# Chunks 16 and 17 of the way down of two feed-forward steps: from plain products to a fifth group of seven block products

## The chip, the cores and the metric

The kernel runs on one core of one Trainium2 chip. The metric is the device time of one launch in microseconds. Three runs of the kernel before took 1115.5, 1116.13 and 1116.92 us; the median, 1116.13, is the time before.

## The reference

One step of a decoder layer over 576 rows: a prompt of 512 and eight samples of 8. All in fp32. The part that is changed is the half-weight feed-forward step, which stands first and last in the layer:

```python
def swiglu(x, w_gate, w_up, w_down):
    return (jax.nn.silu(x @ w_gate) * (x @ w_up)) @ w_down

x = x + 0.5 * swiglu(rmsnorm(x, ffn1_norm), ffn1_w_gate, ffn1_w_up, ffn1_w_down)
...   # input projection, RG-LRU heads, pooling heads, output projection, cross attention
x = x + 0.5 * swiglu(rmsnorm(x, ffn2_norm), ffn2_w_gate, ffn2_w_up, ffn2_w_down)
```

The model width is 1024 (8 blocks of 128), the hidden width 2816 (22 chunks of 128).

## The kernel before

Activations lie transposed: 128 features on the partitions, the 576 rows along the free axis, in two halves of 288. Every fp32 product is made of three products of rounded parts: an operand is split into a high part (a cast on the scalar engine, ACT, line 192) and a low part (the difference, on the vector engine, DVE, line 195), and high x high, high x low and low x high are added up in PSUM. So each weight block costs a load, a cast and a difference before the tensor engine (PE) can use it.

`ffn` (line 374) computes one feed-forward step. `head` is true in the first step. The *way up* makes the 22 hidden chunks, two or three of them plainly, the rest in a loop (line 816), chunk by chunk, by a scheme in which a 2x2 block product takes seven block products where the plain way takes eight. The seven are named 11, E, 22, F, G, 12 and H in the loop; each has twelve matrix products here (`product`, line 367). They accumulate in the PSUM tiles `pu`, `pc`, `pa`. `finish_chunk` (line 800) does the product 22 of a chunk in the middle of the next chunk, or after the loop for the last.

The *way down* multiplies the hidden chunks by `w_down` and adds the result to `x`. Its work is cut into *steps* in a queue (`steps`, line 485), and `fill()` takes one step from that queue behind each of the seven products of a chunk. One product of the way up and one step make what is called a period below. An explicit chain keeps the tensor engine's products in the order in which they are written; the other engines' orders come from a list scheduler that goes by the written order among what it takes to be ready.

For chunks 0 to 15, four groups of four chunks (`quick(g)`, line 629) also use seven block products for eight. In a group, pair `i` (0 to 15 over all groups) covers two output blocks; `depth` two means that the inner dimension of each block product is two chunk pairs deep: `put` makes 2 x 3 products. Its PSUM tiles are `dU`, `dC`, `dA` and `dD`, four banks under the tag `d`. The steps of a pair are `s11`, `sE`, `sF`, `s12`, `sH` and `sG` with `s22`. U takes up 11, is copied to A, takes up F, is copied to D, takes up H, is read out, takes up 22 and is read out again (`take`, line 641). Read-outs go into temporary tiles `add_e` (tag `acc`, one buffer) and `add_1`, `add_2` (tag `sq`, two buffers), and a DMA issued by GpSimd (POOL) adds them to `x` in place (lines 657, 684, 691). `ensure` (line 601) makes the split weight tiles `dh` and `dl` (three buffers) from the raw blocks in `td`, a ring of four slots, and from a fourth block in `t2`; `fetch_pair` (line 586) loads them through the queue of SyncE (SP). In the second step two sums of blocks have been formed ahead, in DRAM; in the first step DVE forms them (lines 613, 614).

The operands of the hidden side are in `pairs` (line 550): `build_a` and `build_b` make, of a pair of chunks, the seven splits that the groups need; `build_plain` makes one plain split of a chunk.

The last six chunks are plain: `PLAIN = (16, 2), (18, 4)`. `down(0)` covers chunks 16 and 17 and is put into the queue at chunk 18, behind the fourth group. It makes eight output blocks times two chunks, a step each, with six products (three parts, two halves) into `pd` (tag `d`). Its panels, 128 x 256, go through `fetch` and `make`. Sixteen steps of it run from the last filler of chunk 19 on. In the first step of the layer the last of them stands behind `finish_chunk` of chunk 21; in the second an additional `fill()` puts it ahead. `down(1)` then does chunks 18 to 21 after the loop, in the first step with the addition to `x` on DVE, in the second in a tail of its own that also makes the final norm. While `down(0)` does its block 7, it already makes panel 0 of the next one (`make(8)`).

Of the kernel before, what the change touches and what calls it, by code (L numbers as in the profile page):

```python
# [9 lines left out]
F32 = mybir.dt.float32  # L10
F32R = mybir.dt.float32r
# [5 lines left out]
P = 128  # L17
# [4 lines left out]
FFC = 22  # L22
STD = (3, 2)

FAST = 4
PLAIN = (16, 2), (18, 4)
NQ = DC // 2
OFFS = [0, P, 2 * P, 3 * P, T - P]
TA = T - P
# [41 lines left out]
def hybrid_step(ctx, tc, a):  # L71
    nc = tc.nc
    v, s, te = nc.vector, nc.scalar, nc.tensor
# [92 lines left out]
    for i in range(FAST * NQ):  # L166
        w = a["f2_d"][i // NQ, i % NQ].rearrange("p b k n -> p b (k n)")
# [21 lines left out]
    def split(hi, lo, src, scale=None):  # L189

        if scale is None:
            i = cast[0] = s.copy(hi, src)  # L192
            if first[0] is not None:
                after_(i, first[0])
            return v.tensor_tensor(out=lo, in0=src, in1=f(hi), op=ALU.subtract)  # L195
        s.activation(hi, src, AF.Copy, scale=scale)
        return v.scalar_tensor_tensor(out=lo, in0=src, scalar=scale, in1=f(hi), op0=ALU.mult, op1=ALU.subtract)
# [176 lines left out]
    def ffn(name, n, fp, turn, plain, head=False):  # L374

        wstd, wgu, wq, wd = (a[f"{name}_{q}"] for q in ("s", "gu", "d", "dp"))

        def single(tag, nm_):  # L380
            return now["ff"].tile([P, 512], F32, tag=tag, bufs={"u": 2, "d": 4}.get(tag, 1), name=nm_)
# [103 lines left out]
        steps = deque()  # L485
# [62 lines left out]
        raw, raw22, pairs, t2 = {}, {}, {}, {}  # L548
# [31 lines left out]

        td = fp.tile([P, 4, 2, P], F32, name="td")

        def slot(i, k):
            return td[:, (i + k) % 4]

        def fetch_pair(i, half):


            if i < FAST * NQ:
                g, q = divmod(i, NQ)  # L590
                if head:
                    for k in range(2 * half, 2 + half):
                        nc.sync.dma_start(slot(i, k), wq[g, q, :, k])
                else:
                    nc.sync.dma_start(slot(i, 3 * half), dsum[g][q][:, half].rearrange("p (k n) -> p k n", n=P))
                    nc.sync.dma_start(slot(i, 1 + half), wq[g, q, :, 1 + half])
                if half == 0:
                    t = draw[i] = fp.tile([P, 2, P], F32, tag="t2", bufs=2, name=f"t2{i}")
                    nc.sync.dma_start(t, wq[g, q, :, 3 * head])

        def ensure(n):

            while made[0] < min(n, 4 * FAST * NQ):
                i, k = divmod(made[0], 4)
                w = [fp.tile([P, 2, 2, P], F32R, tag=tag, bufs=3, name=f"{tag}{i}{k}") for tag in ("dh", "dl")]
                names = (("E", "11"), ("F", "12"), ("H", "G"), ("22",))[k]
                if k == 3:
                    split(*(q[:, 0] for q in w), draw.pop(i))
                else:
                    if k == 1:  # L610
                        v.tensor_add(slot(i, 1), slot(i, 1), slot(i, 0))
                    elif k == 0 and head:
                        v.tensor_add(slot(i, 3), slot(i, 0), slot(i, 1))
                        e = v.tensor_add(slot(i, 0), slot(i, 0), draw[i])
                        if i == 0:
                            after_(e, row_done)
                    j = (i + (0, 1, 3)[k]) % 4
                    if j == 3:
                        names = names[::-1]
                    split(*w, td[:, j:j + 2] if j < 3 else td[:, 0:4:3])  # L620
                    if k == 1:
                        v.tensor_add(slot(i, 0), slot(i, 1), slot(i, 2))
                    if k:
                        fetch_pair(i + 1, k - 1)
                for b, nm_ in enumerate(names):
                    dparts[i, nm_] = [q[:, b] for q in w]
                made[0] += 1

        def quick(g):

            ps = {}

            def put(i, nm_, b, out, start):
                w = dparts.pop((i, nm_))
                for k in range(2):
                    for m, (qw, qx) in enumerate(((0, 0), (0, 1), (1, 0))):
                        mm(out, lhsT=w[qw][:, k, :], rhs=pairs[2 * g + k][qx][:, b, :],
                           start=start and k == 0 and m == 0, stop=k == 1 and m == 2, skip_group_check=True)

            def take(dst, src, sign):  # L640
                taken[0] = s.activation(dst, src, AF.Copy, scale=0.5 * sign)  # L641

            def s11(i):
                ensure(4 * i + 2)
                ps[i] = cols([single("d", q) for q in ("dU", "dC", "dA", "dD")])
                U, C, A, D = ps[i]
                put(i, "11", N11, U, True)
                s.copy(A, U)

            def sE(i):  # L650
                U, C, A, D = ps[i]
                put(i, "E", T1, C, True)
                t = halves(rows.tile([P, T], F32, tag="acc", bufs=1, name="add_e"))
                take(t[:, 0, :], C, -1)
                take(t[:, 1, :], C, 1)
                j = 2 * (i % NQ)
                nc.gpsimd.dma_start(x[:, j:j + 2, HT:], t, accum_op=ALU.add)  # L657

            def sF(i):
                ensure(4 * i + 3)  # L660
                U, C, A, D = ps[i]
                put(i, "F", T2, U, False)
                s.copy(D, U)

            def s12(i):
                U, C, A, D = ps[i]
                put(i, "12", N21, A, False)
                ps[i, 1] = rows.tile([P, T], F32, tag="sq", name="add_1")
                take(ps[i, 1][:, :HT], A, -1)

            def sH(i):
                ensure(4 * i + 4)
                U, C, A, D = ps[i]
                put(i, "H", T3, U, False)
                ps[i, 2] = rows.tile([P, T], F32, tag="sq", name="add_2")
                take(ps[i, 2][:, HT:], U, 1)

            def sG(i):
                ensure(4 * i + 5)
                U, C, A, D = ps[i]  # L680
                put(i, "G", N22, D, False)
                t = ps.pop((i, 1))
                take(t[:, HT:], D, -1)
                nc.gpsimd.dma_start(x[:, 2 * (i % NQ), :], t, accum_op=ALU.add)  # L684

            def s22(i):
                U, C, A, D = ps[i]
                put(i, "22", T4, U, False)
                t = ps.pop((i, 2))
                take(t[:, :HT], U, 1)  # L690
                nc.gpsimd.dma_start(x[:, 2 * (i % NQ) + 1, :], t, accum_op=ALU.add)  # L691

            for i in range(g * NQ, (g + 1) * NQ):
                steps.extend([(q, i) for q in qs] for qs in ((s11,), (sE,), (sF,), (s12,), (sH,), (sG, s22)))

        if head:
            xs = [fp.tile([P, DC * P], F32, tag=tag, bufs=3, name=f"xs_{tag}{i}") for i in range(2) for tag in ("ph", "pl")]
# [99 lines left out]
        def fill():  # L797
            go(1)
# [5 lines left out]

        def build(f):
            p = f // 2
            if p < 2 * FAST:
                if f % 2:
                    build_b(p)
            elif 2 * p + 2 == FFC:  # L810
                build_plain(f)
            elif f % 2:
                build_plain(f - 1)
                build_plain(f)

        for f in range(plain, FFC):
# [4 lines left out]
            if f == plain:  # L821
                if not head:
                    prepare_g(f)
                load_11(f + 2)
            if f == FFC - 5:
                fetch(0)
            fill()
            product(C, w["E"], n, T1, True)
            e1 = small_tile("e1")
# [9 lines left out]
            if before:  # L839
                finish_chunk(before)  # L840
                raw[f - 1] = before[2]
                build(f - 1)
            if f == PLAIN[1][0]:
                down(0)
            prepare_e(f + 1)
            fill()
            if f in range(4, 4 * FAST + 1, 4):
                quick(f // 4 - 1)
            product(U, w["F"], n, T2, False)
            u2 = small_tile("u2")  # L850
            out_[0] = s.copy(u2, U)
# [23 lines left out]
            prepare_g(f + 1)  # L875
            load_11(f + 3)
            raw[f] = g
            if f % 2 and f < 4 * FAST:
                build_a(f // 2)
            if f == 3:  # L880
                ensure(2)
            fill()
            first[0] = None
            before = w, U, g
        if not head:
            fill()
        finish_chunk(before)
        build(FFC - 1)
        gi = len(PLAIN) - 1
# [757 lines left out]
def _inputs(i):  # L1647
# [45 lines left out]
    for n in (1, 2):  # L1693
        gu = np.stack([panels(l0[f"ffn{n}_w_{q}"]) for q in ("gate", "up")], axis=1)
        m = STD[n - 1]
        out[f"f{n}_s"] = gu[:m]

        gu = gu[m:].reshape(FFC - m, 2, P, KP, 2, P).transpose(0, 2, 1, 4, 3, 5)
        out[f"f{n}_gu"] = gu.reshape(FFC - m, P, 4, KP, P)[:, :, [2, 0, 1, 3]]

        order = [2, 0, 1, 3] if n == 1 else [3, 0, 1, 2]
        wd, c = panels(l0[f"ffn{n}_w_down"]), 4 * FAST
        out[f"f{n}_dp"] = wd[:, :, c:]
        wd = wd[:, :, :c].reshape(NQ, 2, P, FAST, 2, 2, P).transpose(3, 0, 2, 1, 5, 4, 6)
        out[f"f{n}_d"] = wd.reshape(FAST, NQ, P, 4, 2, P)[:, :, :, order]
    out["w_in"] = panels(l0["w_in"])
# [49 lines left out]
```

## Time and profile before

| | |
|---|---|
| median of 3 runs | 1116.13 us |
| profiled execution | 1115.27 us, of which the span from first to last instruction 1113.5 us |
| granted tensor-engine clock | 0.998 |
| matrix products | 8310 |
| busy: PE, DVE, ACT, POOL | 1100.5, 881.1, 688.1, 208.1 us |

A row of an engine gives busy time, its share of the span and the number of instructions. Matrix products overlap in the array, so the duration of one is longer than the distance to the next. The chain is the work that ended last, followed back; in order of time its pieces are merged runs of instructions with start and length. In a group's row stand line, engine, operation, output and inputs, shape and count, then the busy time, the mean in ns, and the idle time of that engine ahead of it with what ended it. A wait row gives the total, how often, and the longest. In a table of stretches the columns are PE, PE's weight loads, DVE, ACT and POOL, each busy time with the number of instructions, then clock, share of the transfer engines and GB/s. Landing times run from a DMA's issue to its last byte.

### The profile page before, as it was taken

How to read it: one execution, taken by the hardware profiler on the slowest of the kernel's cores; microseconds unless marked ns; L12 is line 12 of the kernel's file. 1: busy time of each engine (PE TensorE's matmuls, PEld its weight loads, DVE VectorE, ACT ScalarE, POOL GpSimd, SP SyncE). 2: the span in 40 equal slices, each digit the busy share in tenths (PEclk: the TensorE clock that was granted, in tenths of full speed). 3: DMA queues.
4: the chain of work that ended last, by engine and by line, in shares of the span. 5: the costliest groups of instructions: out<-in, count | busy, mean ns of one | idle time of the engine just before them, and what ended most of it. 6: DMA issues, size and time to landing. Idle time of an engine off the chain costs nothing.

```text
span 1113.5 us, 21821 instructions
## 1 busy us (share of the span) xinstructions
PE 1100.5 (99%) x8310; PEld 1078.8 (97%) x8310; DVE 881.1 (79%) x1571; ACT 688.1 (62%) x1285; POOL 208.1 (19%) x246
## 2 busy tenths in 40 slices
PE   9999999999999999999999999999999999999997
PEld 8999999999999999999988889999999999999996
DVE  7899888889866878979865666769888888787755
ACT  8566666676664645786643555446666666666554
POOL 0012222221221024422131000000222222222210
PEclk9999999999999999999999999999999999999999
DMA  9457767776766655577558952233786876867662
GB/s 319 122 131 178 158 155 167 171 171 147 170 139 145 184 160 132 126 209 169 161 167 279 332 196 92 75 98 74 167 181 154 191 170 154 185 152 174 131 155 86
DMA packets 95097, 181.71 MB, mean 163 GB/s; under 512 B 10064, under 2 KB 47184, under 8 KB 94864
## 3 DMA queue, kind: packets, MB, share of 16 engines
q1 hardware_dynamic: 60992, 126.26, 35.3%
q0 software_dynamic: 31472, 51.65, 28.4%
q10 hardware_dynamic: 2528, 2.41, 0.6%
q8 instruction: 65, 1.06, 0.4%
q14 instruction: 40, 0.33, 0.1%
HBM read 142.44 MB, written 13.20 MB: 140 GB/s over the span
## 4 chain that ended last, share of the span: by engine, by line
PE 97%; DMA 1%; ACT 1%; DVE 1%; issue 0%; DVEq 0%; SPq 0%; ACTq 0%
PE pu L149 24%; PE pc L149 11%; PE dU L149 9%; PE pd L149 6%; PE pa L149 5%; PE xo L149 5%; PE wo L149 5%; PE pg L149 4%; PE in_l L149 2%; PE in_p L149 2%; PE in_g L149 2%; PE dC L149 2%; PE dA L149 2%; PE k L149 2%; PE dD L149 2%; PE v L1464 2%
## 5 line engine op out<-in xcount | busy, mean ns | idle before, releaser
L456 POOL DMA_DIRECT2D r<-f_gu x39 | 34.9, 894 | 361.0 <-DVE r L453 197.6
L192 ACT CAST dh<-td 128x512 fp32r<-128x512 f32 x96 | 59.3, 618 | 30.2 <-PE dA L149 14.4
L149 PE MATMUL dU<-ph,dh 128*128 128x288 f32 x256 | 75.7, 296 | 0.9 <-ACT add L641 0.9
L149 PE MATMUL dU<-ph,dl 128*128 128x288 f32 x256 | 75.4, 295 | 0.0
L149 PE MATMUL dU<-pl,dh 128*128 128x288 f32 x256 | 75.4, 295 | 0.0
L195 DVE TENSOR_TENSOR dl<-td,dh 128x512 fp32r<-128x512 f32 x96 | 64.6, 686 | 10.1 <-ACT dh L192 10.0
L195 DVE TENSOR_TENSOR wl_e<-r,wh_e 128x1024 fp32r<-128x1024 f32 x39 | 47.6, 1222 | 29.0 <-ACT wh_e L192 29.0
L657 POOL DMA_DIRECT2D x<-add_e x32 | 38.9, 1214 | 143.3 <-ACT add_e L641 46.4
L192 ACT CAST wh_g<-r 128x1024 fp32r<-128x1024 f32 x39 | 41.0, 1051 | 27.2 <-PE pc L149 13.5
L684 POOL DMA_DIRECT2D x<-add x32 | 30.9, 964 | 138.7 <-ACT add L641 93.7
L195 DVE TENSOR_TENSOR wl_h<-r,wh_h 128x1024 fp32r<-128x1024 f32 x39 | 47.6, 1220 | 3.0 <-ACT wh_h L192 3.0
L149 PEld LDWEIGHTS dU<-ph,dh 128*128 128x128 f32 x256 | 48.1, 188 | 1.4 <-ACT add L641 1.4
L149 PEld LDWEIGHTS dU<-ph,dl 128*128 128x128 f32 x256 | 48.2, 188 | 0.0
L149 PEld LDWEIGHTS dU<-pl,dh 128*128 128x128 f32 x256 | 48.1, 188 | 0.0
L195 DVE TENSOR_TENSOR wl_g<-r,wh_g 128x1024 fp32r<-128x1024 f32 x39 | 47.6, 1221 | 0.3 <-ACT wh_g L192 0.3
L192 ACT CAST wh_h<-r 128x1024 fp32r<-128x1024 f32 x39 | 40.9, 1049 | 10.3 <-PE pu L149 7.2
L192 ACT CAST wh_e<-r 128x1024 fp32r<-128x1024 f32 x39 | 41.1, 1053 | 0.6 <-PE pg L149 0.6
L865 ACT ACTIVATE g<-g 128x576 f32<-128x576 f32 x39 | 26.6, 683 | 23.6 <-DVE g L864 21.9
L691 POOL DMA_DIRECT2D x<-add x32 | 36.8, 1149 | 1.0 <-ACT add L641 0.8
L192 ACT CAST ph<-g 128x576 fp32r<-128x576 f32 (+1 forms) x39 | 22.9, 588 | 18.6 <-DVE g L571 10.5
L830 ACT COPY e<-pc 128x288 f32<-128x288 f32 x39 | 15.6, 401 | 29.3 <-PE pc L149 28.4
L641 ACT ACTIVATE add<-dU 128x288 f32<-128x288 f32 x64 | 26.2, 409 | 12.0 <-PE dU L149 12.0
(677 smaller groups left out, 4616.2 us busy)
## 6 DMA issues: line engine op xcount, KB each, us to landing
x<-add POOLq DMA_DIRECT2D x80, 288.0 KB, 5.6
r<-f_gu SPq DMA_DIRECT2D x39, 512.0 KB, 3.9
r<-f_gu SPq DMA_DIRECT2D x78, 256.0 KB, 3.4
td<-f_d SPq DMA_DIRECT2D x80, 128.0 KB, 5.0
r<-f_gu POOLq DMA_DIRECT2D x39, 256.0 KB, 4.6
x<-add_e POOLq DMA_DIRECT2D x32, 288.0 KB, 4.7
dsum<-f_d POOLq DMA_DIRECT2D x32, 256.0 KB, 5.1
ck<-ck SPq DMA_DIRECT2D x16, 512.0 KB, 5.1
```

Of the source, the lines that this page charges most:

```text
L149: i = te.matmul(*args, **kw)
L192: i = cast[0] = s.copy(hi, src)
L195: return v.tensor_tensor(out=lo, in0=src, in1=f(hi), op=ALU.subtract)
L456: nc.gpsimd.dma_start(r0[:, 0], wgu[f - plain, :, 3], accum_op=ALU.add)
L641: taken[0] = s.activation(dst, src, AF.Copy, scale=0.5 * sign)
L657: nc.gpsimd.dma_start(x[:, j:j + 2, HT:], t, accum_op=ALU.add)
L684: nc.gpsimd.dma_start(x[:, 2 * (i % NQ), :], t, accum_op=ALU.add)
L691: nc.gpsimd.dma_start(x[:, 2 * (i % NQ) + 1, :], t, accum_op=ALU.add)
L830: out_[0] = s.copy(e1, C)
L865: silu = s.activation(g, g, AF.Silu, scale=-1.0)
L1464: te.matmul(ps[:, m, :HD], lhsT=lhs[:, kd, ms], rhs=w[wi][:, k, :], start=kd == 0 and i == 0, stop=kd == DC - 1 and i == 2)
```

## The change

Chunks 16 and 17 leave the plain part and become a fifth group, `quick(4)`, queued at chunk 18 in place of `down(0)`. It has only one pair of chunks, so its block products are one pair deep (`depth(i)` is 1): three products each, 128 columns for a weight block in place of 2 x 128. It has four pairs of output blocks (`i` from 16 to 19). Its steps take two block products each: `s11` with `sE`, `sF` with `s12`, `sH` with `sG`, and `s22` alone. Its raw blocks come from a new input `d2`, and in both layer steps DVE forms their sums. Chunks 16 and 17 go through `build_a` and `build_b` (pair 8) in place of `build_plain`. Four chunks are left plain, as `down(0)`. After the loop, the queue is emptied and the first panel made ahead of `finish_chunk`; the first two panels are fetched at the start of chunk 21.

```diff
-PLAIN = (16, 2), (18, 4)
+NG = FAST + 1
+PLAIN = ((18, 4),)
...
+        def depth(i):
+            return 2 if i < FAST * NQ else 1
+
         def slot(i, k):
-            return td[:, (i + k) % 4]
+            return td[:, (i + k) % 4, :depth(i)]
...
-            if i < FAST * NQ:
+            if i < NG * NQ:
                 g, q = divmod(i, NQ)
-                if head:
+                if head or g == FAST:
+                    w = wq2[q] if g == FAST else wq[g, q]
                     for k in range(2 * half, 2 + half):
-                        nc.sync.dma_start(slot(i, k), wq[g, q, :, k])
+                        nc.sync.dma_start(slot(i, k), w[:, k])
...
-            while made[0] < min(n, 4 * FAST * NQ):
+            while made[0] < min(n, 4 * NG * NQ):
                 i, k = divmod(made[0], 4)
-                w = [fp.tile([P, 2, 2, P], F32R, tag=tag, bufs=3, name=f"{tag}{i}{k}") for tag in ("dh", "dl")]
+                d = depth(i)
+                w = [fp.tile([P, 2, 2, P], F32R, tag=tag, bufs=3, name=f"{tag}{i}{k}")[:, :, :d] for tag in ("dh", "dl")]
...
-                    elif k == 0 and head:
+                    elif k == 0 and (head or d == 1):
                         v.tensor_add(slot(i, 3), slot(i, 0), slot(i, 1))
                         e = v.tensor_add(slot(i, 0), slot(i, 0), draw[i])
...
-                for k in range(2):
+                for k in range(depth(i)):
                     for m, (qw, qx) in enumerate(((0, 0), (0, 1), (1, 0))):
                         mm(out, lhsT=w[qw][:, k, :], rhs=pairs[2 * g + k][qx][:, b, :],
...
-                steps.extend([(q, i) for q in qs] for qs in ((s11,), (sE,), (sF,), (s12,), (sH,), (sG, s22)))
+                turns = ((s11,), (sE,), (sF,), (s12,), (sH,), (sG, s22))
+                if g == FAST:
+                    turns = (s11, sE), (sF, s12), (sH, sG), (s22,)
+                steps.extend([(q, i) for q in qs] for qs in turns)
...
-            if p < 2 * FAST:
+            if p <= 2 * FAST:
                 if f % 2:
                     build_b(p)
...
-            if f == FFC - 5:
+            if f == FFC - 1:
                 fetch(0)
+                fetch(1)
...
-            if f == PLAIN[1][0]:
-                down(0)
             prepare_e(f + 1)
             fill()
             if f in range(4, 4 * FAST + 1, 4):
                 quick(f // 4 - 1)
+            elif f == PLAIN[0][0]:
+                quick(FAST)
...
-            if f % 2 and f < 4 * FAST:
+            if f % 2 and f < PLAIN[0][0]:
                 build_a(f // 2)
...
-        if not head:
-            fill()
+        go(len(steps))
+        make(0)
         finish_chunk(before)
         build(FFC - 1)
```

More of the change, by code (lines that the diff above doesn't have):

```diff
@@ L374, in ffn @@
     def ffn(name, n, fp, turn, plain, head=False):
-        wstd, wgu, wq, wd = (a[f"{name}_{q}"] for q in ("s", "gu", "d", "dp"))
+        wstd, wgu, wq, wd, wq2 = (a[f"{name}_{q}"] for q in ("s", "gu", "d", "dp", "d2"))
         def single(tag, nm_):
@@ L597, in fetch_pair @@
                 if half == 0:
-                    t = draw[i] = fp.tile([P, 2, P], F32, tag="t2", bufs=2, name=f"t2{i}")
-                    nc.sync.dma_start(t, wq[g, q, :, 3 * head])
+                    t = draw[i] = fp.tile([P, 2, P], F32, tag="t2", bufs=2, name=f"t2{i}")[:, :depth(i)]
+                    nc.sync.dma_start(t, wq2[q, :, 3] if g == FAST else wq[g, q, :, 3 * head])
         def ensure(n):
-            while made[0] < min(n, 4 * FAST * NQ):
+            while made[0] < min(n, 4 * NG * NQ):
                 i, k = divmod(made[0], 4)
-                w = [fp.tile([P, 2, 2, P], F32R, tag=tag, bufs=3, name=f"{tag}{i}{k}") for tag in ("dh", "dl")]
+                d = depth(i)
+                w = [fp.tile([P, 2, 2, P], F32R, tag=tag, bufs=3, name=f"{tag}{i}{k}")[:, :, :d] for tag in ("dh", "dl")]
                 names = (("E", "11"), ("F", "12"), ("H", "G"), ("22",))[k]
@@ L611, in ensure @@
                         v.tensor_add(slot(i, 1), slot(i, 1), slot(i, 0))
-                    elif k == 0 and head:
+                    elif k == 0 and (head or d == 1):
                         v.tensor_add(slot(i, 3), slot(i, 0), slot(i, 1))
                         e = v.tensor_add(slot(i, 0), slot(i, 0), draw[i])
-                        if i == 0:
+                        if i == 0 and head:
                             after_(e, row_done)
@@ L619, in ensure @@
                         names = names[::-1]
-                    split(*w, td[:, j:j + 2] if j < 3 else td[:, 0:4:3])
+                    split(*w, (td[:, j:j + 2] if j < 3 else td[:, 0:4:3])[:, :, :d])
                     if k == 1:
@@ L634, in put @@
                 w = dparts.pop((i, nm_))
-                for k in range(2):
+                for k in range(depth(i)):
                     for m, (qw, qx) in enumerate(((0, 0), (0, 1), (1, 0))):
                         mm(out, lhsT=w[qw][:, k, :], rhs=pairs[2 * g + k][qx][:, b, :],
-                           start=start and k == 0 and m == 0, stop=k == 1 and m == 2, skip_group_check=True)
+                           start=start and k == 0 and m == 0, stop=k == depth(i) - 1 and m == 2, skip_group_check=True)
             def take(dst, src, sign):
@@ L1702, in _inputs @@
         wd, c = panels(l0[f"ffn{n}_w_down"]), 4 * FAST
-        out[f"f{n}_dp"] = wd[:, :, c:]
+        out[f"f{n}_dp"] = wd[:, :, c + 2:]
+        q = wd[:, :, c:c + 2].reshape(NQ, 2, P, 1, 2, P).transpose(0, 2, 1, 4, 3, 5)
+        out[f"f{n}_d2"] = q.reshape(NQ, P, 4, 1, P)[:, :, [2, 0, 1, 3]]
         wd = wd[:, :, :c].reshape(NQ, 2, P, FAST, 2, 2, P).transpose(3, 0, 2, 1, 5, 4, 6)
```

## The prediction

> **What bounds the kernel now.** I read the page's parts on busy time and on the chain first, then the chain in order of time around the end of both feed-forward steps, then the tensor engine's waits, then stretches of the vector and scalar engines, and last the landing times of transfers.
>
> ```profile
> span 1113.5 us, 21821 instructions
> PE 1100.5 (99%) x8310; PEld 1078.8 (97%) x8310; DVE 881.1 (79%) x1571; ACT 688.1 (62%) x1285; POOL 208.1 (19%) x246
> PE 97%; DMA 1%; ACT 1%; DVE 1%; issue 0%; DVEq 0%; SPq 0%; ACTq 0%
> L149 PE MATMUL dU<-ph,dh 128*128 128x288 f32 x256 | 75.7, 296 | 0.9 <-ACT add L641 0.9
> ```
>
> The tensor engine carries 97% of the chain, so a product taken away is worth its place on that engine. How much that is, the group's 296 ns does not say: products overlap. The chain in time has the true pitch. In the first step it reads, for the last filler steps:
>
> ```profile
> 327.57 0.79 PE pd L149 x6
> 328.36 1.59 PE pu L149 x12
> ...
> 356.97 1.60 PE pa L149 x12
> ...
> 360.90 0.69 DVE dl L195
> 361.60 0.38 DVE e L871
> 361.98 0.04 issue
> 362.02 1.86 PE pu L149 x12
> ```
>
> Twelve products take 1.59 us and six 0.79: 0.1325 us each. From 327.57 on, `pd` is the plain work on chunks 16 and 17 (`down(0)`): one filler step of six products behind each twelve of the way up, 2.385 us a period. Chunk 20 begins at 328.36, chunk 21 seven periods later. In the second step the same place has no gap:
>
> ```profile
> 1073.48 1.59 PE pu L149 x12
> 1075.07 1.58 PE pd L149 x12
> 1076.64 1.59 PE pu L149 x12
> ```
>
> The waits of the tensor engine that bear on this:
>
> ```profile
> PE dU L149 <- ACT add L641: 0.9, 2, 0.6
> PE pu L149 <- DVE e L871: 0.3, 1, 0.3
> ```
>
> The second row is the gap before 362.02. The twelve products end at 363.88 (362.02 + 1.86), and without it they would have ended 1.59 us after 361.74 (356.97 + 1.60, then 0.79, 1.59 and 0.79), at 363.33. So it costs 0.55 us: 0.27 of waiting, and a restart, since 1.90 us run from the releaser's end (361.98) to the end of twelve products that else take 1.59: 0.31 us. I use 0.31 for every restart.
>
> **The change part by part.**
>
> *Products removed.* `down(0)` has 8 output blocks x 2 chunks x 6 = 96 products of 288 columns in each step. The fifth group has 4 pairs x 7 block products x 3 = 84 of the same shape. 12 fewer in each step, 24 in all, at 0.1325 us: 3.18 us less. (At the group's 296 ns it would be 7.1 us; that is the wrong column.) [...]
>
> *Filler steps.* `down(0)` made 16 steps of six products. The group makes four a pair, 16 again: three of six products and one (`s22` alone) of three. They start in the same slot (last of chunk 19), one is left over after chunk 21, and both before and after it is the last. The periods become 2.385 three times and 1.99 once.
>
> *The last step.* It moves ahead of `finish_chunk`, alone: `s22` of pair 19 adds into U, which the scalar engine must first read out behind `sH`, and between the two stand only `sG`'s three products (0.40 us). Before, a period's twelve lay between. These rows price the read-out:
>
> ```profile
> L530 ACT ACTIVATE add<-pd 128x288 f32<-128x288 f32 x14 | 4.9, 404 | 0.3 <-PE pd L149 0.3
> L192 ACT CAST dh<-wr_d 128x256 fp32r<-128x256 f32 x7 | 2.9, 407 | 1.4 <-DMA wr_d<-f_dp 1.4
> L192 ACT CAST wh<-r 128x512 fp32r<-128x512 f32 x2 | 1.2, 622 | 2.5 <-PE pc L149 1.9 <-PE pu L149 0.6
> ```
>
> If the scalar engine is free, 0.404 us after `sH` ends against 0.40 of cover: nothing but the restart, 0.31 us in each step, 0.62 in all. The bounds: nothing (the read-out overlaps enough), and 0.31 + 0.62 when the 512-wide cast of `make(0)` is ahead of it. I take 0.31: that cast's buffer is free from `s12` on, a period earlier, and chunk 21 leaves the scalar engine room (below). In return the 0.55 us of the first step goes: the addition `e` (L871) now has the leftover step and its wait as well as the last filler, some 1.5 us where 0.79 was short, and the 0.69 us `dl` ahead of it comes from `make(8)`, which is no more. Late next is `make(0)`'s pair of weights for the following `down`: its cast and difference, 0.62 and 0.69 (next fence), fit into `finish_chunk`'s 1.59 us, as the low half is read 0.53 us later still. Cover gone, they cost at most 0.7.
>
> *Scalar and vector work.* The prices:
>
> ```profile
> L195 DVE TENSOR_TENSOR dl<-wr_d,dh 128x256 fp32r<-128x256 f32 x7 | 2.9, 421 | 2.7 <-ACT dh L192 2.6
> L195 DVE TENSOR_TENSOR dl<-wr_d,dh 128x512 fp32r<-128x512 f32 x2 | 1.4, 693 | 2.0 <-ACT dh L192 2.0
> L648 ACT COPY dA<-dU x32: 383/383/426, 65.4 to 1027.5; 128x288 f32<-128x288 f32 x32
> ```
>
> A 128-wide operation isn't in these rows; by the slope from 512 to 256 I estimate 0.30 us for a cast and 0.285 for a difference or a sum. Each pair of output blocks now needs, on ACT, three casts of 256 and one of 128, two copies and six read-outs: 4.71 us, where two panels needed 2.43. On DVE it is four differences and four sums, 2.69 us for 0.84. So seven periods gain 1.75 x 2.28 = 4.0 us on ACT and 1.75 x 1.85 = 3.2 on DVE. The stretches (busy columns in the order PE, PEld, DVE, ACT):
>
> ```profile
> 294.20:311.00 16.80, 16.80 (x130) 16.80 (x129) 15.00 (x27) 11.50 (x24) 3.89 (x5) 1.00 0.71 156
> 328.40:345.00 16.60, 16.60 (x127) 16.60 (x126) 11.45 (x20) 9.60 (x20) 2.61 (x3) 1.00 0.66 135
> 345.00:361.70 16.70, 16.70 (x127) 16.49 (x125) 7.77 (x14) 7.44 (x19) 3.46 (x4) 1.00 0.67 155
> ```
>
> Chunk 20 (second row) goes to DVE 14.7 and ACT 13.6 of 15.9 us, 92% and 86%; chunk 21 to 11.0 and 11.4. Chunk 18 (first row) runs at DVE 89% and ACT 68% with the tensor engine never waiting. So it fits on average, hidden by the products; ACT's 86% has no precedent. What is exposed is queueing. U is read out four times a pair; behind `sE` to `s22` a read-out has 1.99 us of slack (0.40 + 1.59), behind `s22` only 1.59, three times a step. In chunk 20 a 576-wide cast stands there:
>
> ```profile
> 336.27 0.67 ACT L192 CAST ph<-g 128x576 fp32r<-128x576 f32 x1
> 336.84 0.70 ACT L530 ACTIVATE add<-pd 128x288 f32<-128x288 f32 x2
> ```
>
> It waited for a panel load that is gone; without that it starts near 335.3, the read-out behind it ends near 336.3, and U is wanted at 336.65. One such wait costs at most about 0.4 + 0.31 = 0.7. Low end 0, high end 0.7 at each of six places (4.2 us). The first wait row above is this very wait, 0.9 us in 32 pairs, so I stay near the low end: 0.2 a step, 0.4 in all.
>
> `build_a` and `build_b` for pair 8 replace two plain splits: three more casts and differences and four sums of 288 columns, in chunks 17 and 18, as they stand in chunks 13 and 14 for pair 6: no cost of their own, since that pattern's only waits are the 0.9 us above.
>
> *Transfers.* Group 4 loads four blocks of 64 KB a pair on SP, in place of two panels of 128 KB. Each is asked for two or more periods (4.8 us) ahead, the first row below being the nearest, and from chunk 20 on no way-up load stands ahead of them on SP. If late, DVE's two sums wait, with two more periods before the product. POOL issues 12 accumulations into x instead of 8. The first four groups issue L684 and L691 a microsecond apart; the new spacing, two microseconds and more, lies between that and L531's, which stands alone:
>
> ```profile
> t<-f_d SPq DMA_DIRECT2D x1, 128.0 KB, 3.2
> q0 software_dynamic: 2112, 3.44, 46.4%
> q0 software_dynamic: 1152, 2.36, 38.9%
> L531 POOL DMA_DIRECT2D x<-add x16: 850/858/882, 331.8 to 1077.7; - x16
> DMA to landing us min/median/max: 3.4/4.1/5.5
> L684 POOL DMA_DIRECT2D x<-add x32: 847/908/1241, 79.1 to 1040.1; - x32
> DMA to landing us min/median/max: 3.5/5.2/6.5
> L691 POOL DMA_DIRECT2D x<-add x32: 859/1038/1562, 80.4 to 1041.1; - x32
> DMA to landing us min/median/max: 4.4/6.6/8.0
> ```
>
> A `sq` buffer comes round after 6.77 us (1.59, 0.80, 1.59, 0.80, 1.59, 0.40) instead of four periods, 9.5. Read-out 0.4, POOL's start 0.4 later (0.40 at 310.18, then 310.99 below), landing L: free after 0.8 + L, in time while L is under 6.0. I take 5.2, L684's median, between the other two: no cost, which holds for every L below it; L691's medians and worst are the rival below.
>
> ```profile
> 310.18 0.40 ACT L641 ACTIVATE add<-dD 128x288 f32<-128x288 f32 x1
> 310.99 0.87 POOL L684 DMA_DIRECT2D x<-add  x1 [5.88 <-ACT add L641]
> ```
>
> *Sum.* -3.18 - 0.55 + 0.62 + 0.4 = -2.7 us. The profiled execution took 1115.27 us (span 1113.5, 1.8 around it), so 1112.6 by its own time; it lies 0.86 under the median of 1116.13, and against that median the forecast is 1113.4.
>
> **The rivals.**
>
> *Queueing eats it.* Half-size operations keep ACT and DVE at 86% and 92% in chunk 20, and U's read-outs come late at four or more of the six places: 4 x 0.7 = 2.8 instead of 0.4, total -0.3 us, 1115.8: no change. For it: ACT's share is new, and its instructions run in order. Against: the pattern at 89% DVE lost 0.9 us in 32 pairs, and chunk 21 is light. [...]
>
> *Landing decides: slower.* If accumulations land at L, U's read-out behind `sH` waits L - 5.97 us for its buffer. The tensor engine has 1.99 - 0.44 = 1.55 us of slack before `s22`, and then pays the rest and 0.31. Eight accumulations filled 38.9% of the transfer engines in the plain work's 35 us, so twelve fill about 58%; the first four groups stood at 46.4% and their L691 at a median of 6.6. In proportion, L is 8.3, and each of six turnovers pays 1.1: 6.6 us, 1120.0. It makes the kernel slower from an L of 8.0 on, and costs nothing up to 7.5. For it: that share. Against: the issues are no longer packed, and way-up loads are gone.
>
> *The work is hidden better than I think.* The leftover read-out and the pinch cost nothing: -3.7 us, 1112.4.
>
> **How the numbers follow.** A measurement of this kernel tells about 0.2%, 2.2 us, from no change. The forecast (gains of 1.7 to 3.8, the best case in it) has 0.60, and I put 0.49 of that over 2.2. Queueing 0.26, all within the bound. Landing 0.10, 0.08 of it slower and 0.02 within. Instructions ordered otherwise elsewhere in the program, 0.04, half of it each way. Faster 0.51, within 0.39, slower 0.10. The forecast's own range is 1112.0 to 1114.6. The range for 8 in 10 runs from the best case less half a microsecond of run spread, 1111.9, through queueing to part of the landing case, 1117.4.
>
> **What would show it.** Right: 8286 matmuls; form `dU<-ph,dh` at x288, `pd<-ph,dh` at x72; pitch 1.59 and 0.40 for the three-product step; the row `pu <- DVE e L871` gone; a short `dU <- ACT add` wait before the last `s22` of each step. Wrong: tensor-engine waits on ACT or DVE in chunks 20 and 21 that sum to over 1.5 us; ACT waiting on x's transfers; a pitch of three-product groups above 0.1325; or new waits in the tail, where `make(0)` comes later than `make(8)` did.

## The result, and the profile after

The changed kernel takes 1118.11 us (median of 22 runs, 1115.56 to 1124.98), the kernel before 1115.68 in the same runs. The ratio is 1.0025, with a 95% interval of 1.0016 to 1.0034: slower by 2.4 us, where 2.7 less had been forecast. The profiled execution took 1120.83 us, 2.7 above its median, so it shows the loss larger than it is on average. The spread is itself part of the result: before, the runs lie within 4 us, after, within 9.5.

The page of the changed kernel, its head and two of the groups:

```profile
span 1119.0 us, 22000 instructions
PE 1098.9 (98%) x8286; PEld 1075.3 (96%) x8286; DVE 895.9 (80%) x1633; ACT 702.6 (63%) x1339; POOL 217.5 (19%) x254
L150 PE MATMUL dU<-ph,dh 128*128 128x288 f32 x288 | 86.1, 299 | 6.6 <-ACT add L647 6.5
L619 DVE TENSOR_TENSOR td<-td 128x256 f32<-128x256 f32 (+1 forms) x24 | 9.1, 379 | 50.1 <-DMA td<-f_d 50.0
```

The 24 products are gone (8310 to 8286). But the tensor engine now waits 6.5 us for read-outs in front of `dU`, where it waited 0.9, and the vector engine waits 50.0 us for raw blocks, where it waited 25.5, as the row of the kernel before has it. (Read-outs are line 647 here, the sums 619 and 620, the accumulations of `add_e`, `add_1` and `add_2` 663, 690 and 697.)

```profile
DVE td L613 <- DMA td<-f_d: 25.5, 9, 5.3
```

Where in the program it was lost can be read from two landmarks of each feed-forward step: the first block product of its first group (`dU`) and the last product of its way down (`pd`). In the views by tile, first for the kernel before and then for the changed one, the last two numbers before the semicolon are the first and last start:

```profile
L149 PE MATMUL dU<-ph,dh x114: 291/294/401, 63.8 to 297.6; 128*128 128x288 f32 x114
L149 PE MATMUL pd<-ph,dl x96: 288/296/313, 327.9 to 389.9; 128*128 128x288 f32 x96
L149 PE MATMUL dU<-ph,dh x60: 292/294/302, 781.0 to 898.1; 128*128 128x288 f32 x60
L149 PE MATMUL pd<-ph,tl x24: 365/366/367, 1083.4 to 1097.5; 128*128 128x448 f32 x24
```

```profile
L150 PE MATMUL dU<-ph,dh x114: 291/295/406, 64.2 to 298.3; 128*128 128x288 f32 x114
L150 PE MATMUL pd<-ph,dl x64: 288/295/313, 368.4 to 393.2; 128*128 128x288 f32 x64
L150 PE MATMUL dU<-ph,dh x58: 292/294/302, 783.8 to 896.1; 128*128 128x288 f32 x58
L150 PE MATMUL pd<-ph,tl x24: 362/366/368, 1088.3 to 1102.3; 128*128 128x448 f32 x24
```

So in the changed kernel the first step lasts 329.0 us from the one to the other (393.2 - 64.2), the part between the steps 390.6 and the second step 318.5. Before, the same landmarks give 326.1, 391.1 and 316.5. The forecast's terms come to -1.6 in the first step and -1.1 in the second; the profile shows +2.9 and +2.0. The rest of the program is unchanged. A profile is one execution: the stretch from the first landmark to the last start of `dU` ahead of 300 us (64.2 to 298.3 above), which is the same in the changed kernel and all its variants below, lasts from 233.2 to 234.7 us in their profiles. So differences of about 1 us between two profiles say little.

**The first step.** The timelines of DVE, ACT and the tensor engine, and of SyncE's queue, at the beginning of the fifth group (start, length, and in brackets the idle time before and what ended it):

```profile
314.14 2.02 SPq L598 DMA_DIRECT2D td<-f_d  x3
...
321.90 0.29 DVE L619 TENSOR_TENSOR td<-td 128x128 f32<-128x128 f32 x1 [6.58 <-DMA td<-f_d]
...
322.43 1.22 DVE L196 TENSOR_TENSOR wl_e<-r,wh_e 128x1024 fp32r<-128x1024 f32 x1
...
326.37 1.05 ACT L193 CAST wh_g<-r 128x1024 fp32r<-128x1024 f32 x1 [3.06 <-DVE r L473]
...
327.32 0.40 ACT L647 ACTIVATE add<-dU 128x288 f32<-128x288 f32 x1
...
327.78 0.40 PE L150 MATMUL dU<-ph,dh 128*128 128x288 f32 x1 [1.86 <-ACT add L647]
```

The first two sums of pair 16 stand in DVE's order ahead of the way-up work of chunk 20 (`wl_e`, and then the differences `r`). Their blocks, asked for from 314.14 on, are there at 321.90; the slowest of the three transfers took 7.2 us from issue to landing. DVE had come to the first sum at 315.32 and stands still for 6.58 us; `r` is late, so ACT's cast `wh_g` is late, the read-out of U stands behind that cast, and the tensor engine waits 1.86 us, for a read-out of the *old* group's pair 15, which has no need of these sums.

Then the granted clock falls. A table of two stretches behind that wait, with the columns of the prediction's:

```profile
328.20:329.00 0.80, 0.80 (x8) 0.80 (x8) 0.80 (x1) 0.66 (x2) 0.27 (x1) 1.00 0.09 20
329.00:332.40 3.40, 3.40 (x16) 3.40 (x16) 3.18 (x8) 2.56 (x6) 1.48 (x2) 0.50 0.60 114
```

For 3.4 us the clock is 0.50: 16 products start where some 26 fit (3.40 / 0.1325): 1.3 us by the products that are missing, 1.7 by half of the 3.4. The waits for read-outs around the fifth group, in this step from 318 to 372 us and in the second from 1035 to 1086, are:

```profile
PE dU L150 <- ACT add L647: 2.2, 2, 1.9
```

```profile
PE dU L150 <- ACT add L647: 2.9, 2, 1.7
```

So of the first step's shortfall of 4.5 us (from -1.6 to +2.9), 2.2 are waits, 0.3 the restart behind the long one, and 1.3 to 1.7 the clock; of the second's 3.1 (from -1.1 to +2.0), 2.9 are waits, in this execution without a fall of the clock.

**The second step.** Its last pairs, in the timelines of POOL and ACT, and then in the chain in order of time:

```profile
1068.54 1.21 POOL L663 DMA_DIRECT2D x<-add_e  x1 [1.27 <-ACT e L840]
...
1071.57 0.41 ACT L647 ACTIVATE add<-dD 128x288 f32<-128x288 f32 x1
...
1072.77 0.42 ACT L647 ACTIVATE add<-dU 128x288 f32<-128x288 f32 x1
...
1074.97 0.91 POOL L690 DMA_DIRECT2D x<-add  x1 [5.22 <-ACT dA L654]
1075.54 1.22 POOL L697 DMA_DIRECT2D x<-add  x1
```

```profile
1075.54 4.78 DMA x<-add
...
1080.40 0.42 ACT add L647
...
1080.87 0.66 PE dU L150 x3
```

`add_1` is read out by 1071.98, but its accumulation (line 690) goes out at 1074.97, 0.6 us after that of `add_e` has landed (issued at 1068.54, landed 5.8 us later). Both add to the same part of `x`, and here the second goes out only when the first has landed. In none of the eight pairs of the fifth group, four in each step, does `add_1` go out earlier: it stands 0.6 to 1.2 us behind that landing. `add_2`, read out by 1073.19, stands behind `add_1` in POOL's order and goes out at 1075.54 (line 697). Its landing takes 4.78 us more, and only then is there a `sq` buffer for the last read-out of U. The row of line 690 names ACT's copy `dA` as the releaser; that the landing is what POOL waits for is shown by a run below. The waits of ACT in this part (1035 to 1086):

```profile
ACT dh L193 <- DVE td L620: 5.7, 3, 3.3
ACT wh_g L193 <- DVE r L473: 2.3, 1, 2.3
ACT add L647 <- DMA x<-add: 1.5, 2, 0.8
```

Two delays meet here: late sums (first two rows) and late buffers (third). For pair 16 it is as in the first step. From pair 17 on, the sums are late since a pair's blocks are loaded only when the pair before has left its slots of the ring (SyncE's loads at line 598 wait 3.3 us for DVE's `dl` in the first step and 2.8 in the second), and land some 4 us after that (medians of 3.9 and 4.0).

### The profile page after: what moved, and what is told of

Read it like the earlier page. It is cut to its first block, busy times and chain, and to the rows that moved or that the text cites. A ratio compares the mean times of both kernels' runs of the same rounds, so it can differ in the third digit from the quotient of the medians.

```text
span 1119.0 us, 22000 instructions
## 1 busy us (share of the span) xinstructions
PE 1098.9 (98%) x8286; PEld 1075.3 (96%) x8286; DVE 895.9 (80%) x1633; ACT 702.6 (63%) x1339; POOL 217.5 (19%) x254
## 5 line engine op out<-in xcount | busy, mean ns | idle before, releaser
L193 ACT CAST dh<-td 128x512 fp32r<-128x512 f32 (+1 forms) x120 | 69.1, 575 | 43.4 <-DVE td L620 17.5
L150 PE MATMUL dU<-ph,dh 128*128 128x288 f32 x288 | 86.1, 299 | 6.6 <-ACT add L647 6.5
L150 PE MATMUL dU<-pl,dh 128*128 128x288 f32 x288 | 85.0, 295 | 0.0
L150 PE MATMUL dU<-ph,dl 128*128 128x288 f32 x288 | 85.0, 295 | 0.0
L196 DVE TENSOR_TENSOR dl<-td,dh 128x512 fp32r<-128x512 f32 (+1 forms) x120 | 74.5, 631 | 10.5 <-ACT dh L193 9.7
L663 POOL DMA_DIRECT2D x<-add_e x40 | 48.6, 1216 | 161.4 <-ACT add_e L647 56.9
L690 POOL DMA_DIRECT2D x<-add x40 | 39.0, 976 | 147.6 <-ACT add L647 79.6
L150 PEld LDWEIGHTS dU<-pl,dh 128*128 128x128 f32 x288 | 54.3, 189 | 0.0
L619 DVE TENSOR_TENSOR td<-td 128x256 f32<-128x256 f32 (+1 forms) x24 | 9.1, 379 | 50.1 <-DMA td<-f_d 50.0
L697 POOL DMA_DIRECT2D x<-add x40 | 46.7, 1167 | 7.2 <-ACT dh L193 4.3
L647 ACT ACTIVATE add<-dU 128x288 f32<-128x288 f32 x80 | 32.7, 409 | 13.5 <-PE dU L150 10.9
```

The costliest lines, as they stand in the source:

```text
L150: i = te.matmul(*args, **kw)
```

## The experiments

Theory A: the raw blocks arrive late, and what stands behind DVE's waiting sums pays. Theory B: the accumulations into `x` wait for each other, so the buffer of the read-outs comes round late. Theory C, the prediction's rival: ACT and DVE are simply too full. The first four kernels take A away in two ways, B alone, and all at once; four more leave one edit out of the whole; two test a mechanism and a term. The table has them all; "first", "between" and "second" are the landmark distances of each profile in us.

| kernel | median us (runs) | ratio to before, 95% | first | between | second |
|---|---|---|---|---|---|
| before | 1115.9 (33) | | 326.1 | 391.1 | 316.5 |
| changed | 1118.11 (22) | 1.0025, 1.0016 to 1.0034 | 329.0 | 390.6 | 318.5 |
| pin_sums | 1117.15 (12) | 1.0011, 1.0000 to 1.0022 | 327.1 | 393.4 | 317.2 |
| ring_split | 1119.48 (12) | 1.0033, 1.0021 to 1.0045 | 327.2 | 393.4 | 318.2 |
| e_bufs | 1117.38 (11) | 1.0011, 1.0001 to 1.0021 | 324.0 | 391.5 | 319.3 |
| all_three | 1113.28 (10) | 0.9974, 0.9964 to 0.9985 | 324.0 | 391.1 | 315.3 |
| no_bufs | 1117.72 (11) | 1.0017, 1.0009 to 1.0026 | 326.4 | 393.7 | 316.3 |
| no_ring | 1114.64 (12) | 0.9998, 0.9987 to 1.0010 | 325.4 | 390.8 | 315.7 |
| no_pin | 1114.58 (11) | 0.9988, 0.9979 to 0.9998 | 324.2 | 391.1 | 316.4 |
| no_spq | 1114.72 (12) | 0.9988, 0.9977 to 0.9998 | 324.8 | 392.0 | 315.3 |
| drop_e | 1113.57 (12) | 0.9977, 0.9968 to 0.9987 | 324.5 | 394.1 | 315.2 |
| tail_only | 1115.07 (1) | | 325.7 | 391.3 | 316.5 |

Each kernel ran beside runs of the kernel before, whose medians were 1115.68 to 1115.93; the ratios are against these.

**pin_sums**: the first sums of the fifth group stand behind the latest way-up operation of DVE.

```diff
-                        v.tensor_add(slot(i, 3), slot(i, 0), slot(i, 1))
+                        e = v.tensor_add(slot(i, 3), slot(i, 0), slot(i, 1))
+                        if d == 1:
+                            after_(e, pin[0])
...
-            v.tensor_mul(g[:, HT:], e1, g[:, HT:])
+            pin[0] = v.tensor_mul(g[:, HT:], e1, g[:, HT:])
```

> Edit: each of the four first sums of group 4 on the vector engine is ordered behind the latest finished step of the way up, so that it can no longer stand in front of work that the way up needs. Theory A (the sums stand too early in the vector engine's order, wait for raw blocks that have not landed, and hold the scalar engine's casts and read-outs behind them): the 1.9 us wait of the tensor engine before the last s22 of group 3 in the first step goes, and most of the 1.7 us in the second; total wait of dU on the read-outs falls from 6.5 us to 3 or less; 2 to 4 us off the 1118.1, so 1114 to 1116. Theory B (read-outs wait for a buffer whose accumulation into x has not landed): no change, 1117.5 to 1118.5, the dU waits stay at 6 us. Theory C (half-size operations simply fill the scalar and vector engines): no change or slower.

It takes back about 1 us of the median, where theory A expected 2 to 4, and its interval overlaps that of the changed kernel. Theory A's signs are there in part: the wait of 1.86 us is gone with the half clock behind it (1.00 from 311 to 345), the waits before `dU` fall from 6.5 to 3.2 us in all, and the first step is 1.9 us shorter. In each of the two steps ACT still waits 6.5 us for the sums: the pin settles who stands behind them, not when the blocks come.

**ring_split**: the pairs of the fifth group alternate between the two halves of the ring's width, so a pair's blocks needn't wait for the slots of the pair before.

```diff
-            return td[:, (i + k) % 4, :depth(i)]
+            h = i % 2
+            return td[:, (i + k) % 4] if depth(i) == 2 else td[:, (i + k) % 4, h:h + 1]
```

> Edit: pairs 16 to 19 take turns in the two halves of the ring of raw blocks (group 4 uses only one half of its width), so that the blocks of pair i+1 need not wait until pair i's are split. Theory A: the vector engine's wait for raw blocks falls from 12.5 us to about 7 in the first step (only the one for pair 16 stays), the tensor engine's wait in chunk 20 of the second step goes, the one at pair 16 in the first step stays; 1 to 3 us off, 1115 to 1117. Theory B: no change. Theory C: no change.

A miss: no faster, if anything slower. DVE's wait for raw blocks in the first step falls only from 12.5 to 10.4 us, where about 7 was expected. Two rows of ACT's waits give a likely reason, the first from this kernel, the second from the changed one:

```profile
ACT add L648 <- DMA x<-add: 5.6, 8, 1.2
```

```profile
ACT add L647 <- DMA x<-add: 2.3, 3, 0.8
```

With earlier blocks, the read-outs run into the late buffers eight times instead of three. That one wait took the other's place is argued, not shown: in this profile the two steps together are 2.1 us shorter than in the changed kernel, and its loss lies between them.

**e_bufs**: `add_1` of pairs 17 to 19 goes into another set of buffers, so that only `add_2` takes turns in `sq`. The order of instructions on every engine stays that of the changed kernel.

```diff
-                ps[i, 1] = rows.tile([P, T], F32, tag="sq", name="add_1")
+                ps[i, 1] = full_tile("add_1") if i > FAST * NQ else rows.tile([P, T], F32, tag="sq", name="add_1")
```

> Edit: the temporary add_1 of pairs 17 to 19 is taken from the three wide tiles of the way up instead of the two that add_1 and add_2 share, so no read-out has to wait for an accumulation to land. Theory B: the scalar engine's waits on accumulations into x (0.8 us in the first step, 1.5 in the second) go, and with them the 1.2 us wait before the last s22 of the second step and whatever hangs on it in other runs: 1.5 to 4 us off, 1114 to 1116.5. Theory A: at most the one wait at the end, 1.2 + 0.3 us: 1116.5 to 1118. Theory C: no change.

About 0.7 us of the median, as theory A alone had it (1116.5 to 1118) and less than theory B's 1.5 to 4; the interval overlaps that of the changed kernel. In its profile the first step is 5.0 us shorter than the changed kernel's (324.0), the second 0.8 longer (319.3): there the sums are late, the tensor engine waits 1.8 us once, and the clock is 0.90 over the 17 us around it (1044 to 1061), as it is in the changed kernel from 328 to 345 with its 3.4 us at half clock.

**all_three**: the three edits together, and the panel fetches of the last part stand behind the raw blocks in SyncE's queue.

```diff
-                nc.sync.dma_start(fetched[i], wd[j, :, c0:c0 + fg, :])
+                q = nc.sync.dma_start(fetched[i], wd[j, :, c0:c0 + fg, :])
+                if loaded[0] is not None:
+                    after_(q, loaded[0])
...
-                        nc.sync.dma_start(slot(i, k), w[:, k])
+                        loaded[0] = nc.sync.dma_start(slot(i, k), w[:, k])
```

> Edit: the three edits together, and the panels for the plain chunks ordered behind the raw blocks on SyncE's queue. Theories A and B together: tensor-engine waits in chunks 19 to 21 of both steps under 1.5 us in all, 1112.4 to 1114, 2 to 3 us faster than the kernel before. Theory C: no better than 1117.

1113.28 us: 2.65 less than before and 4.8 less than the changed kernel, the fastest version here, as theories A and B together had it, with as many products and as many operations on DVE and ACT as the changed kernel. From its page, its waits and its stretches:

```profile
span 1110.8 us, 21989 instructions
...
PE dU L150 <- ACT add L653: 0.8, 2, 0.5
DVE td L623 <- DMA td<-f_d: 25.4, 9, 5.3
328.40:344.30 15.90, 15.90 (x122) 15.90 (x121) 13.59 (x31) 12.75 (x32) 4.25 (x4) 1.00 0.87 186
```

DVE's wait for raw blocks is back at the old groups' 25 us, ACT waits for a transfer of `x` only once, 0.6 us and for `add_e`, and in chunk 20 DVE works 13.59 and ACT 12.75 of 15.9 us with the tensor engine never idle. That is the answer to C: the load is there, and it fits.

**no_bufs**: all_three without the extra read-out buffers.

> The version of all_three without the extra read-out buffers (pinned sums, two half rings, panel fetches behind the raw blocks; add_1 back in the two sq buffers). Theory B (a read-out buffer comes round late because the accumulation into x waits for the landing of the one before it): all_three's 1113.3 us plus 1.2 us at the end of each step, where U's read-outs took turns with a late buffer in the changed kernel, so about 1115.7, with rows in which ACT's add waits for x's transfer, and a wait of the tensor engine for that read-out of 1 us or more. Rival (only the raw blocks matter): 1113.3, and waits of the tensor engine for read-outs stay under 1 us in all.

Theory B, and by more than expected: 4.4 us of the median, the whole way back to the changed kernel's neighbourhood (the intervals 1.0009 to 1.0026 and 0.9964 to 0.9985 are far apart). Its chain in the first step runs twice through an accumulation, both times that of `add_2` (line 703 here), which goes out 0.6 us behind that of `add_1` (line 696), and ACT's row over the whole run says the same:

```profile
337.64 5.83 DMA x<-add
...
343.55 0.42 ACT add L653
...
344.01 0.67 PE dU L150 x3
...
347.58 0.54 POOL x L696
...
348.16 6.58 DMA x<-add
...
354.82 0.42 ACT add L653
...
355.28 0.67 PE dU L150 x3
```

```profile
ACT add L653 <- DMA x<-add: 10.3, 7, 2.4
```

**drop_e**: no_bufs, with the accumulation of `add_e` left out in the fifth group; those parts of `x` are not added.

```diff
-                nc.gpsimd.dma_start(x[:, j:j + 2, HT:], t, accum_op=ALU.add)
+                if i < FAST * NQ:
+                    nc.gpsimd.dma_start(x[:, j:j + 2, HT:], t, accum_op=ALU.add)
```

> The version no_bufs (pinned sums, two half rings, panel fetches behind the raw blocks, add_1 in the two sq buffers) with the four accumulations of add_e left out in the fifth group of both steps: those parts of x are not added. If a read-out buffer comes late because the accumulation of add_1 first waits for the landing of add_e's on the same rows of x, then without it add_1's goes out at once, lands some 5 us later, the buffer is free after 0.8 + 5 us as the prediction had it, under its 6.77, and the time is all_three's 1113.3 us less nothing; ACT waits for no transfer of x. Rival (add_1's own landing is too long, whatever stands before it): ACT still waits for transfers of x over 3 us a step and the time stays above 1116.5.

1113.57 us with two `sq` buffers: as fast as all_three. The second half of `add_1`'s read-out and its accumulation, from the timelines of ACT and POOL, here:

```profile
1068.46 0.41 ACT L653 ACTIVATE add<-dD 128x288 f32<-128x288 f32 x1
...
1069.23 0.85 POOL L697 DMA_DIRECT2D x<-add  x1 [6.60 <-ACT add L653]
```

It goes out 0.77 us after the read-out starts, as the prediction had it (0.8), where it was 3.4 us in the changed kernel (1071.57 to 1074.97). In no_bufs it is the late buffers of `add_2` that reach the tensor engine, in the chain above. In pairs 16 and 17 there, `add_2` goes out 1.4 to 2.2 us after its read-out starts and takes 5.5 to 6.6 us to land; here it is 0.8 us, and 4.0 to 4.2. So it is `add_e`'s accumulation, and not the length that the others have by themselves, that makes the buffers late: it holds `add_1` back, and then the two go out 0.6 us apart, where here over 2 us lie between them. The run takes the hold, the crowding and the traffic of `add_e` away at once, and doesn't price them one by one.

**no_ring**, **no_pin**, **no_spq**: all_three without one of the other three edits.

> The version of all_three with the one ring of four slots (pinned sums, panel fetches behind the raw blocks, extra read-out buffers). Theory A (raw blocks land late because the next pair's load waits for the last use of the slot by the pair before): DVE still waits over 8 us for raw blocks beyond the old groups' 25 us, and half of the gain over the changed kernel is lost: 1115.5 us. Rival (the order of the sums is enough, with buffers): 1113.3, DVE's waits on raw blocks may stay, but reach nobody.

> The version of all_three without the pinned order of the first sums (two half rings, panel fetches behind the raw blocks, extra read-out buffers). If early placement of the sums in DVE's order matters only because the blocks are late, the two half rings (blocks a pair ahead) make the pin needless: 1113.3 us. If the placement itself is the loss, DVE waits at the sums of pair 16, whose first blocks no ring can bring sooner, then ACT and the tensor engine in chunk 20: some 2 us in the first step, 1115.5.

> The version of all_three without the rule that panel fetches stand behind the raw blocks in SyncE's queue (pinned sums, two half rings, extra read-out buffers). Panels of the next part then go between raw blocks and take a place in the queue; with the loads a pair ahead this should reach nobody: 1113.3 us. If SyncE's order is a term of its own, DVE waits on raw blocks again near chunk 21 and the time is over 1114.5.

Each is 1.3 to 1.4 us slower than all_three by the median. The intervals of no_pin and no_spq overlap all_three's, and that of no_ring only just doesn't, so the single prices are not settled. no_ring lies nearer to theory A's 1115.5 than to its rival's 1113.3, but DVE waits only 4 us more for raw blocks than in all_three, where over 8 had been expected, and of the 1.4 us by which its first step is longer, 0.8 fall ahead of the fifth group, where it changes nothing. no_pin lies between its two expectations: its loss is in the second step (316.4 for 315.3), not in the first, where it had been placed; there ACT waits 3.3 us once for a sum. no_spq's profile has 0.9 us more than all_three in the part between the steps and 0.8 more in the first step ahead of the fifth group, and it changes no instruction in either place: for SyncE's order as a term of its own, this shows nothing.

**tail_only**: the kernel before, with the leftover filler step of the first step ahead of `finish_chunk`.

```diff
-        if not head:
-            fill()
+        fill()
         finish_chunk(before)
```

> The kernel before, with the one leftover filler step of the first feed-forward step put ahead of the last product 22, as the second step has it. The prediction's term of 0.55 us: the wait for the addition e at the end of the first step goes, and from the first block product of the way down to the last product of that step the profile takes 0.5 to 0.6 us less than the 326.1 us of before. Rival: the wait stays, since the difference ahead of that addition is still there; 326.1 us.

The chain in order of time, from the one run of this kernel:

```profile
357.13 1.58 PE pa L149 x12
...
361.10 1.58 PE pd L149 x12
362.68 1.59 PE pu L149 x12
```

The gap is gone. The last twelve end at 364.27; `pa` began 0.16 us later than before (357.13 for 356.97), and one step of 0.79 has moved ahead: 364.27 - 0.16 - 0.79 = 363.32, where it was 363.88. That is 0.56 us for the 0.55 forecast; the landmarks, read to a tenth, give 0.4.

## Why the prediction was wrong

*Products removed: right.* 8286 products, `dU<-ph,dh` at x288. Twelve take 1.58 us and three 0.40 in all_three's chain, from 1068.07 on:

```profile
1068.07 1.58 PE pa L150 x12
1069.65 0.40 PE dU L150 x3
...
1072.04 0.42 PE dU L150 x3
...
1072.48 0.42 ACT add L653
...
1072.94 0.66 PE dU L150 x3
```

*The last step: right.* The `sH` product ends at 1072.46; with the 0.40 of cover and 0.40 for the last three the engine would be done at 1073.26, and is at 1073.60 (1072.94 + 0.66): 0.34 us, with 0.31 forecast. The 0.55 us came as said, in the one run of tail_only.

*Scalar and vector work: fits, as said.* 13.59 and 12.75 us in a chunk for the forecast 14.7 and 13.6. The forecast was 1 us high, about half of it because it added to busy times of a 16.6 us stretch, not of a chunk of 15.9. A sum of 128 columns takes 0.29 us, as estimated. The 0.4 for pinched read-outs isn't seen in all_three: its two waits before `dU`, 0.8 us, stand in the old groups, as the 0.9 us of the kernel before did, and none in the fifth.

*Transfers: this step failed, twice.*

The first time in "If late, DVE's two sums wait, with two more periods before the product". It priced the wait by the one who uses the sum, and took the 4.8 us between asking and using from the tensor engine's order. DVE came to the first sum of pair 16 only 1.2 us after its first load was issued (315.32 for 314.14), waited 6.58 us, and the tensor engine 1.86 for it. For while DVE waited, all that stood behind that sum was held: way-up differences, then ACT's casts (ACT stood idle 3.06 us for `r`, ahead of `wh_g`), then U's read-out of another pair. The two periods of the one who uses the sum were no cover for these. Taking the waits away from behind the way-up work (the pin) and bringing the blocks sooner (ring, queue) brought, at a guess from the medians that the intervals don't settle, some 1.3 us each where the buffers were there; without them the pin brought 1 us and the ring none.

The second time in "free after 0.8 + L, in time while L is under 6.0". In the median L was right: 4.6 and 4.7 us in the two steps of the changed kernel, where 5.2 was taken. The 0.8 was wrong. `add_1` is issued behind the landing of `add_e`'s accumulation on the same part of `x`, and `add_2` behind `add_1`, so their buffers are held for the rest of that landing too, then for their own, which took up to 6.6 us where the two went out together. From the start of the read-out to the landing of `add_2` it was 2.77 + 4.78 = 7.55 us in the changed kernel (from 1072.77 on), and 1.77 + 5.83 = 7.60 and 2.20 + 6.58 = 8.78 in no_bufs, all above the 6.77 of the buffer's round. In the old groups four periods (9.5 us) lie between `sE` and `sG`, which complete the two read-outs, and the landing is over by then (in the kernel before the two issues lie 5.8 to 12.0 us apart, the second 1.1 us or more behind the landing); with two block products a step it is two periods (4.8 us), about one landing. The traces show the order: 5.1 to 6.4 us from one issue to the next in the changed kernel, never ahead of the landing, and 0.77 from the read-out where the earlier one is left out. Read beside the change, that order puts two accumulations in line behind a third in each of the four pairs of a step, where eight were single.

The two failures don't add up, they hide each other: with either of them left in, most of the loss stays (no_bufs 1117.72, e_bufs 1117.38), and the forecast gain stands only without both (1113.28, -2.65 against before; forecast -2.7).

*The rivals.* "Queueing eats it" is out. "Landing decides" named the place, ACT waiting for transfers of `x`, and the sign; its mechanism, slower landings on busier transfer engines (8.3 us), is not what happened, since their median stayed under 5 us; the 6.58 us on no_bufs' chain is of an accumulation that had been held back. Its price of 6.6 us was above the 2.4 measured.

*What stays open*: the separate prices of the pin, the ring and SyncE's order, those of the hold and of the longer landing behind it, and how much of the 2.4 us is waiting and how much the half clock that can follow it.

## What to carry to other kernels

Price a wait by what stands behind it on the waiting engine, not by the slack of the one who needs the result. Time a buffer's round from the last read-out to the landing *and* ask what the transfer must wait for before it is issued: here the accumulations on one destination ran in series (5.1 to 6.4 us from one issue to the next). And where two waits cover each other, taking away either shows little; take both away before you judge either.

## What the runs showed of the hardware

Behind a wait of the tensor engine of 0.8 to 1.9 us a stretch at half clock followed in four of the profiles. In the changed kernel, behind the wait of 1.86 us, it is 3.4 us long (0.50 from 329.0 to 332.4, and 1.00 on both sides). In e_bufs the clock is 0.90 over the 17 us around the wait of 1.8 us: 1.7 us of missing clock, as 3.4 us at half would make. In no_bufs and drop_e the stretch stands between the two steps, in code that is the same in all of these kernels, behind a wait of 0.8 and 0.9 us, in no_bufs with ten products of one column each in between. The clock there is 0.52 over 3.4 us and 0.98 over the next 3.2 in no_bufs, and 0.54 over 3.4 us and 0.97 over the next 4.6 in drop_e: 1.7 us missing in both. Wait and stretch together account for most of the 2.6 and 3.0 us by which their "between" is longer than all_three's. The profiled runs of these two lie 1.4 and 3.0 us above their medians, so most of their runs are likely without it. pin_sums and ring_split wait 0.8 and 1.0 us at the same place, and their "between" is 393.4 us; no row shows their clock there. From no_bufs, the ten products with the wait ahead of them, and the stretch at half clock (here 0.52 over the window):

```profile
544.20 1.27 PE L150 MATMUL k<-ones,acc_nx 128*128 128x1 f32 x10 [0.84 <-ACT t_nx L1325]
```

```profile
545.40:548.80 3.40, 3.40 (x18) 3.40 (x18) 2.78 (x7) 1.52 (x3) 0.53 (x1) 0.52 0.25 54
```

no_spq has such a wait (0.8 us), and its "between" is 0.9 us above all_three's, which leaves little room for such a stretch. None stands behind the 1.7 us in the second step of the changed kernel or the 1.9 us in the first of no_bufs (clock 1.00 over the 17 us around each), so it doesn't always follow. What brings it on and what sets its length these runs do not show. Since such a stretch fell into code that no edit touches, the distances between landmarks tell more here than the spans.
